# Tying a weight sum behind the previous quad's wide low part in a seven-product matmul block

## The chip, the cores and the metric

The kernel runs on one core of a Trainium2 chip. The metric is the device time of one launch in microseconds (us), the median of several runs. The five engines are named as in the profile: PE (TensorE; its weight loads have a row of their own, PEld), DVE (VectorE), ACT (ScalarE), POOL (GpSimd) and SP, which only issues transfers here.

## The reference

One decoder layer on a sequence of 512 tokens of width 2048, all in float32. What matters for the change is the large input projection of the normalised tokens u, and the output projection of the two branches h_a and h_b:

```python
u = _rmsnorm(h, norm_w)
proj = jnp.matmul(u, w_in)
...
y_a = jnp.matmul(h_a, w_out[:ML_WIDTH])
y_b = jnp.matmul(h_b, w_out[ML_WIDTH:])
return jax.nn.sigmoid(gate_a) * y_a + jax.nn.sigmoid(gate_b) * y_b
```

Between the two stand the mLSTM branch (8 heads) and the gated DeltaNet branch (16 heads), both chunked; the change does not touch them.

## The kernel before, in words

**Split products.** A float32 product is made of three matmuls of a narrower kind: each operand is split into a high part (a cast on ACT, line 140) and a low part (source minus high part, on DVE, line 143), and PE adds high·high, high·low and low·high. So each weight tile passes ACT, then DVE, before PE can finish with it.

**Seven-product blocks.** `seven_stage` (from line 484) computes the product of 512 tokens with 1024 weight columns by a Strassen-Winograd scheme with seven products instead of eight. `SEVEN` lists 13 such blocks of w_in, which run first; `OUTS` lists two of w_out, near the end. A block works through 16 *quads* of weights: A0 to A7 in its first part, B0 to B7 in its second. A quad is one raw tile of three 128x512 weight pieces (`wr3`, three buffers), loaded through SP.

- An A quad needs sums of its pieces (lines 519 and 520 in `first_sums`, on DVE): `t13`, two pieces wide, and `ts`, one piece. `ts` and the first raw piece are split singly (narrow splits), `t13` is split as one tile of 128x1024 (the wide split). `ts` is also sent to DRAM (`t2_d`, line 533, POOL), to come back as the third piece of the B quad with the same number.
- A B quad needs one sum, `ts` (line 537 on DVE), which is split narrowly, and its first two raw pieces are split as the wide tile. The sum waits for all three pieces of the quad.

Of the wide parts (`w2h`, `w2l`) there are two buffers, of `ts` three, of the narrow parts four. In B the products of a quad run in the order m1, m5, m7; m1 and m5 use the wide parts, m7 the narrow ones. Only at a block's end they run B6.m1, B6.m5, B7.m1, B7.m5, B6.m7, B7.m7. Each product is 2 x 3 matmuls (t = 0 and 1; lines 577 to 579).

**Between the parts.** In A the products m6, m1, m5, m7 are gathered in PSUM. When A7 is done with one of them, it is taken out: m6 by ACT (`copy1`, line 562), the others by DVE additions into the tile X (`add`, line 631): U1 = m6 + m1, C22 = U1 + m5, C22 = C22 + m7, each for t = 0 and 1, six additions. B goes on in the banks of m1, m5 and m7, so each product of B0 waits for the addition that reads its bank.

**What sets the order.** PE keeps the order in which the code is written. On the other engines a scheduler orders the instructions by priority and by when it thinks that they are ready; each engine then runs its list strictly in that order, and an instruction that waits holds up everything behind it. `behind("V")` binds an instruction on DVE to come after the newest low part (`newest["V"]`, set in `split_lo`). `prep_sums(q)` writes the sum and the narrow splits of quad q, `prep_pair(q)` its wide split; both are called one quad ahead of the products.

Of the kernel before, what the change touches and what calls it, by code (L numbers as in the profile page):

```python
# [11 lines left out]
ALU = mybir.AluOpType  # L12
# [46 lines left out]
def hybrid_body(  # L59
# [18 lines left out]
    V, A, G, T = nc.vector, nc.scalar, nc.gpsimd, nc.tensor  # L78
# [66 lines left out]
    def behind(eng):  # L145

        return tc.issue_after(newest[eng])
# [332 lines left out]
    def seven_stage(sbp, su, s4, X, t2_d, w_, k0, blocks, sinks, hook, queue):  # L480
# [26 lines left out]
        def split(src, wide):  # L507
            if wide:
                hi, lo = (sbp.tile([P, 2, NO], F32R, tag=f"w2{n}", name=f"w{n}", bufs=2) for n in "hl")
            else:  # L510
                hi, lo = (wp.tile([P, 1, NO], F32R, tag=f"w{n}", name=f"w{n}", bufs=NSPL) for n in "hl")
            split_hi(hi, src)
            split_lo(lo, src, hi)
            return [(hi[:, n, :], lo[:, n, :]) for n in range(2 if wide else 1)]

        def first_sums(r):
            ts = wp.tile([P, 1, NO], F32, tag="tg", name="ts", bufs=3)
            t13 = sbp.tile([P, 2, NO], F32, tag="t13", name="t13")
            V.tensor_tensor(out=t13, in0=r[:, 1:3, :], in1=r[:, 0:2, :], op=ALU.subtract)
            V.tensor_tensor(out=ts[:, 0, :], in0=r[:, 2, :], in1=t13[:, 0, :], op=ALU.subtract)  # L520
            return ts, t13

        def prep_sums(q):

            if q >= len(quads) or q in partq:
                return
            _, c1, c2, b, g, i = quads[q]
            r = rawq[q]
            with tc.high_priority(offset=2 * PRIO):
                if g == "A":  # L530
                    ts, t13 = sums.pop(q) if q in sums else first_sums(r)
                    p_ = split(ts, False)
                    queue.dma_start(t2_d[b % 2, i], ts[:, 0, :])  # L533
                    partq[q] = (p_ + split(r[:, 0:1, :], False), t13)
                else:
                    ts = wp.tile([P, 1, NO], F32, tag="tg", name="ts", bufs=3)
                    V.tensor_tensor(out=ts[:, 0, :], in0=r[:, 0, :], in1=r[:, 2, :], op=ALU.subtract)  # L537
                    partq[q] = (split(ts, False), r[:, 0:2, :])

        def prep_pair(q):  # L540
# [23 lines left out]
        def seven(n0, kind, c1, c2):  # L564
# [20 lines left out]
            for n in range(N - 2):  # L585
                prep_sums(n0 + n + 1)
                prep_pair(n0 + n + 1)
                load_quad()
                for m in range(4 if n < KH else 3):
                    if n == N - 3 and m == 2:  # L590
                        prep_sums(n0 + N - 1)
                        prep_pair(n0 + N - 1)
                    product(n, m)
# [3 lines left out]
            for n, m in ((N - 2, 0), (N - 2, 1), (N - 1, 0), (N - 1, 1), (N - 2, 2), (N - 1, 2)):  # L597
                if (n, m) == (N - 2, 1):
                    prep_sums(n0 + N)
                if (n, m) == (N - 1, 0):  # L600
                    prep_pair(n0 + N)
                    load_quad()
                if last and (n, m) == (N - 1, 1):
                    hook()
                product(n, m)
# [1159 lines left out]
```

## Time and profile before

| | us |
|---|---|
| median of 3 runs | 2181.37 (2178.75 to 2184.76) |
| the profiled execution, its own time | 2172.99 |
| its span, first to last instruction | 2171.2 |
| first seven-product matmul of the 13 blocks | 124.1 |
| first seven-product matmul of the two blocks of w_out | 1957.6 |

The granted clock of PE was 0.999 over the span. In the lines that follow, PEld rows are weight loads of PE, one ahead of each matmul; a row of the timeline has start, duration, engine, line, operation, written tile <- read tiles and shape, and in brackets how long the engine sat idle before it and what ended that. Rows of waits have the sum in us, the number of waits and the longest. All times of the traces are counted from the first instruction.

### The profile page before, as it was taken

What the parts mean: (1) busy time and instruction counts of PE and PEld (TensorE: products, weight loads), DVE (VectorE), ACT (ScalarE), POOL (GpSimd) and SP (SyncE); (2) the same over time, 40 slices, a digit from 0 to 9 for tenths busy, and PEclk for the clock granted to TensorE, in tenths of its full rate; (3) what the DMA queues carried; (4) which work ended last, traced back from release to release, by engine and by line L of the source; (5) the groups of instructions that cost most, each with busy time, mean ns of one, the idle gap of its engine ahead of it and who ended that gap; (6) DMA issues with size and microseconds to landing.
All of it is one profiled execution on the core that took longest, in us unless ns stands there. A gap on an engine that the chain in (4) does not pass through costs nothing. (4 is left out here: it accounts for less than half of the span.)

```text
span 2171.2 us, 31926 instructions
## 1 busy us (share of the span) xinstructions
PE 2131.3 (98%) x10544; PEld 1756.0 (81%) x10544; DVE 1715.0 (79%) x2973; ACT 1035.5 (48%) x1994; POOL 432.0 (20%) x651
## 2 busy tenths in 40 slices
PE   6999999999999999999999999999999999999998
PEld 5888888888788887878878888888888888887786
DVE  5887788788788778777866887887887878668877
ACT  5444444444444444444445546456455464435345
POOL 0000000000004000000003335234243263243211
PEclk9999999999999999999999999999999999999999
DMA  5456676667668766766766767677686677778886
GB/s 160 124 185 202 195 213 199 213 199 226 198 222 245 242 191 219 242 186 222 257 197 172 196 173 184 169 181 185 178 222 171 165 185 209 198 239 266 232 281 242
DMA packets 447143, 444.20 MB, mean 205 GB/s; under 512 B 197121, under 2 KB 303842, under 8 KB 446850
## 3 DMA queue, kind: packets, MB, share of 16 engines
q1 hardware_dynamic: 377618, 337.22, 54.1%
q0 software_dynamic: 24752, 72.90, 10.8%
q10 hardware_dynamic: 44608, 32.06, 4.6%
q8 instruction: 82, 1.34, 0.3%
q14 instruction: 83, 0.68, 0.1%
HBM read 348.66 MB, written 97.58 MB: 206 GB/s over the span
## 5 line engine op out<-in xcount | busy, mean ns | idle before, releaser
L140 ACT CAST wh<-wr 128x512 fp32r<-128x512 f32 (+1 forms) x522 | 373.2, 717 | 415.4 <-PE pj L258 231.4
L143 DVE TENSOR_TENSOR wl<-wr,wh 128x512 fp32r<-128x512 f32 (+1 forms) x522 | 437.4, 840 | 109.3 <-ACT wh L140 103.7
L257 PE MATMUL pj<-uh,wh 128*128 128x512 f32 x896 | 376.0, 420 | 0.0
L259 PE MATMUL pj<-uh,wl 128*128 128x512 f32 x896 | 350.8, 391 | 0.0
L258 PE MATMUL pj<-ul,wh 128*128 128x512 f32 x896 | 350.2, 391 | 0.0
L578 PE MATMUL ps<-wl,uh 128*128 128x512 f32 x752 | 295.0, 392 | 4.8 <-DVE wl L143 4.8
L577 PE MATMUL ps<-wh,uh 128*128 128x512 f32 x752 | 294.5, 392 | 4.1 <-DVE X L631 3.5
L579 PE MATMUL ps<-wh,ul 128*128 128x512 f32 x752 | 292.8, 389 | 0.0
L140 ACT CAST wh<-ts 128x512 fp32r<-128x512 f32 x240 | 148.2, 617 | 250.9 <-DVE ts L537 197.8
L140 ACT CAST wh<-t 128x1024 fp32r<-128x1024 f32 x120 | 126.4, 1054 | 275.7 <-PE ps L579 165.7
L577 PE MATMUL ps<-wh,suh 128*128 128x512 f32 x624 | 242.9, 389 | 1.5 <-ACT to L642 1.5
L533 POOL DMA_DIRECT2D t_d<-ts x104 | 56.6, 544 | 936.9 <-DVE ts L520 883.0
L578 PE MATMUL ps<-wl,suh 128*128 128x512 f32 x624 | 242.8, 389 | 0.0
L579 PE MATMUL ps<-wh,sul 128*128 128x512 f32 x624 | 242.7, 389 | 0.0
L259 PEld LDWEIGHTS pj<-uh,wl 128*128 128x128 f32 x896 | 168.3, 188 | 37.3
L257 PEld LDWEIGHTS pj<-uh,wh 128*128 128x128 f32 x896 | 169.0, 189 | 30.0
L258 PEld LDWEIGHTS pj<-ul,wh 128*128 128x128 f32 x896 | 169.2, 189 | 28.1
L143 DVE TENSOR_TENSOR wl<-ts,wh 128x512 fp32r<-128x512 f32 x240 | 163.7, 685 | 35.2 <-ACT wh L140 35.2
L143 DVE TENSOR_TENSOR wl<-t,wh 128x1024 fp32r<-128x1024 f32 x120 | 146.8, 1224 | 55.9 <-ACT wh L140 55.0
L578 PEld LDWEIGHTS ps<-wl,uh 128*128 128x128 f32 x752 | 141.1, 188 | 40.7 <-DVE wl L143 12.7
L577 PEld LDWEIGHTS ps<-wh,uh 128*128 128x128 f32 x752 | 141.1, 188 | 40.1 <-DVE X L631 10.8
L537 DVE TENSOR_TENSOR ts<-wr 128x512 f32<-128x512 f32 x120 | 82.8, 690 | 104.2 <-DMA wr<-t_d 86.1
(334 smaller groups left out, 3826.2 us busy)
## 6 DMA issues: line engine op xcount, KB each, us to landing
wr<-in_w_in_dram SPq DMA_DIRECT2D x744, 256.0 KB, 3.8
wr<-in_w_out_dram SPq DMA_DIRECT2D x138, 256.0 KB, 5.0
t_d<-ts POOLq DMA_DIRECT2D x104, 256.0 KB, 3.9
wr<-t_d SPq DMA_DIRECT2D x104, 256.0 KB, 3.9
xt<-in_x_dram SPq DMA_DIRECT2D x8, 512.0 KB, 7.1
tg_d<-X ACTq DMA_DIRECT2D x16, 256.0 KB, 6.9
tg_d<-to ACTq DMA_DIRECT2D x16, 256.0 KB, 6.0
v<-v_d SPq DMA_DIRECT2D x8, 512.0 KB, 5.8
```

The costliest lines, as they stand in the source:

```text
L140: newest["A"] = A.copy(hi, src).ins
L143: newest["V"] = V.tensor_tensor(out=lo, in0=src, in1=hi.bitcast(F32), op=ALU.subtract).ins
L257: T.matmul(ps[j], hi[:, k, wsl], uh[:, kt, :], start=(kt == 0), stop=False)
L258: T.matmul(ps[j], hi[:, k, wsl], ul[:, kt, :], start=False, stop=False)
L259: T.matmul(ps[j], lo[:, k, wsl], uh[:, kt, :], start=False, stop=(kt == KT - 1))
L533: queue.dma_start(t2_d[b % 2, i], ts[:, 0, :])
L537: V.tensor_tensor(out=ts[:, 0, :], in0=r[:, 0, :], in1=r[:, 2, :], op=ALU.subtract)
L577: T.matmul(ps[t], ah, hi, start=(g == "A" and i == 0), stop=False, skip_group_check=True)
L578: T.matmul(ps[t], ah, lo, start=False, stop=False, skip_group_check=True)
L579: T.matmul(ps[t], al, hi, start=False, stop=(i == KH - 1), skip_group_check=True)
```

## The change

The line that sums the pieces of a B quad is put under `behind("V")`. When it is written, the newest low part is that of the wide split of the quad in front of it (of A7 for B0, of B0 for B1, and so on), so the sum can no longer come ahead of that one in DVE's list.

```diff
                 else:
                     ts = wp.tile([P, 1, NO], F32, tag="tg", name="ts", bufs=3)
-                    V.tensor_tensor(out=ts[:, 0, :], in0=r[:, 0, :], in1=r[:, 2, :], op=ALU.subtract)
+                    with behind("V"):
+                        V.tensor_tensor(out=ts[:, 0, :], in0=r[:, 0, :], in1=r[:, 2, :], op=ALU.subtract)
                     partq[q] = (split(ts, False), r[:, 0:2, :])
```

The lists of PE and SP stay word for word the same (line numbers behind the sum grow by one: the sum is L538 after, the addition L632). On POOL one load of stage-two gates changes places with one load of the last block's operand. On DVE and ACT rows move in each of the 15 blocks, and nowhere else.

DVE from the end of A to the start of B in the third block, before. The raw tiles wr3_2737, wr3_2783, wr3_2821 and wr3_2867 are the quads B0, B1, B2 and B3; X_517 is the tile of the six additions:

```order
L537 TENSOR_TENSOR ts_2857<-wr3_2783 128x512
L143 TENSOR_TENSOR wl_2860<-ts_2857,wh_2859 128x512
L143 TENSOR_TENSOR wl_2818<-wr3_2737,wh_2817 128x1024
L537 TENSOR_TENSOR ts_2889<-wr3_2821 128x512
L631 TENSOR_TENSOR X_517<-X_517,ps_2468 128x512
L631 TENSOR_TENSOR X_517<-X_517,ps_2469 128x512
L631 TENSOR_TENSOR X_517<-X_517,ps_2470 128x512
L143 TENSOR_TENSOR wl_2892<-ts_2889,wh_2891 128x512
L631 TENSOR_TENSOR X_517<-X_517,ps_2471 128x512
L631 TENSOR_TENSOR X_517<-X_517,ps_2472 128x512
L537 TENSOR_TENSOR ts_2921<-wr3_2867 128x512
L631 TENSOR_TENSOR X_517<-X_517,ps_2473 128x512
```

The same place on DVE, after:

```order
L143 TENSOR_TENSOR wl_2818<-wr3_2737,wh_2817 128x1024
L538 TENSOR_TENSOR ts_2857<-wr3_2783 128x512
L632 TENSOR_TENSOR X_517<-X_517,ps_2468 128x512
L632 TENSOR_TENSOR X_517<-X_517,ps_2469 128x512
L632 TENSOR_TENSOR X_517<-X_517,ps_2470 128x512
L143 TENSOR_TENSOR wl_2860<-ts_2857,wh_2859 128x512
L632 TENSOR_TENSOR X_517<-X_517,ps_2471 128x512
L632 TENSOR_TENSOR X_517<-X_517,ps_2472 128x512
L632 TENSOR_TENSOR X_517<-X_517,ps_2473 128x512
L143 TENSOR_TENSOR wl_2864<-wr3_2783,wh_2863 128x1024
L538 TENSOR_TENSOR ts_2889<-wr3_2821 128x512
L143 TENSOR_TENSOR wl_2896<-wr3_2821,wh_2895 128x1024
```

Before, the sum of B2 stood ahead of the six additions and the sum of B3 among them; now only B1's sum is ahead of them, and B1's wide low part follows right behind them.

ACT at the same place, before (copies of line 562 are `copy1`):

```order
L140 CAST wh_2813<-ts_2811 128x512
L140 CAST wh_2859<-ts_2857 128x512
L140 CAST wh_2817<-wr3_2737 128x1024
L562 COPY X_517<-ps_2466 128x512
L562 COPY X_517<-ps_2467 128x512
L140 CAST wh_2891<-ts_2889 128x512
```

ACT at the same place, after:

```order
L140 CAST wh_2813<-ts_2811 128x512
L140 CAST wh_2817<-wr3_2737 128x1024
L563 COPY X_517<-ps_2466 128x512
L563 COPY X_517<-ps_2467 128x512
L140 CAST wh_2859<-ts_2857 128x512
```

The cast of B1's sum stood ahead of B0's wide cast and of the two copies; now it is behind them.

DVE at the end of the same block, before. wr3_2963, wr3_2995 and wr3_3027 are B6, B7 and the next block's A0:

```order
L537 TENSOR_TENSOR ts_3043<-wr3_2995 128x512
L143 TENSOR_TENSOR wl_3046<-ts_3043,wh_3045 128x512
L143 TENSOR_TENSOR wl_3024<-wr3_2963,wh_3023 128x1024
L519 TENSOR_TENSOR t13_3070<-wr3_3027 128x1024
L520 TENSOR_TENSOR ts_3069<-wr3_3027,t13_3070 128x512
L143 TENSOR_TENSOR wl_3050<-wr3_2995,wh_3049 128x1024
```

The same place, after:

```order
L143 TENSOR_TENSOR wl_3024<-wr3_2963,wh_3023 128x1024
L538 TENSOR_TENSOR ts_3043<-wr3_2995 128x512
L519 TENSOR_TENSOR t13_3070<-wr3_3027 128x1024
L143 TENSOR_TENSOR wl_3046<-ts_3043,wh_3045 128x512
L520 TENSOR_TENSOR ts_3069<-wr3_3027,t13_3070 128x512
L143 TENSOR_TENSOR wl_3050<-wr3_2995,wh_3049 128x1024
```

The sum of B7 and its narrow low part, which were ahead of B6's wide low part, now stand behind it, between it and B7's own.

## The prediction

> **What bounds the kernel now.** I read the page first, then the waits of the weight loads, then the timeline where these waits fall. First the busy time of PE and of its weight loads, and three groups of the page: the matmul group whose mean I use, and the two groups of weight loads that wait.
>
> ```profile
> span 2171.2 us, 31926 instructions
> PE 2131.3 (98%) x10544; PEld 1756.0 (81%) x10544; DVE 1715.0 (79%) x2973; ACT 1035.5 (48%) x1994; POOL 432.0 (20%) x651
> ...
> L579 PE MATMUL ps<-wh,sul 128*128 128x512 f32 x624 | 242.7, 389 | 0.0
> ...
> L578 PEld LDWEIGHTS ps<-wl,uh 128*128 128x128 f32 x752 | 141.1, 188 | 40.7 <-DVE wl L143 12.7
> L577 PEld LDWEIGHTS ps<-wh,uh 128*128 128x128 f32 x752 | 141.1, 188 | 40.1 <-DVE X L631 10.8
> ```
>
> PE is taken all the time, and PEld, too, has only 19% of the span free. How fast a block runs when nothing is late shows in the windows view of the weight loads for one of the 13 blocks (columns: stretch, its length, busy time and count, clock, DMA share, GB/s):
>
> ```profile
> 742.00:818.00 76.00, 62.90 (x336) 1.00 0.68 220
> ```
>
> A block is 336 matmuls, so this one ran in 76.0 us, 0.226 us from load to load, of which a load takes 0.19 and 0.04 is the usual gap. A matmul takes 0.389 us by its row, so consecutive ones overlap. Now who makes the blocks wait, first by matmuls, then by weight loads (sum in us, count, longest):
>
> ```profile
> PE ps L578 <- DVE wl L143: 5.2, 12, 0.9
> PE ps L577 <- DVE X L631: 3.5, 6, 1.4
> ```
>
> ```profile
> PEld ps L578 <- DVE wl L143: 13.5, 23, 1.4
> PEld ps L577 <- DVE X L631: 11.5, 18, 1.9
> ```
>
> The two differ by almost three. A matmul counts as busy until its modelled end, 0.389 us, though the next could follow after 0.226; a wait shorter than 0.16 us vanishes, and a longer one loses 0.16. The loads show every one, so I sum by them. The Trainium skill, Perfetto Trace Analysis, section Identifying the Most-Contended Engine, says that matmul busy time is a poor measure of headroom, since matmuls are pipelined, and names LDWEIGHTS busy time instead; the trace agrees (98% against 81%). By the matmul rows the whole prize would be 5.2 + 3.5 = 8.7 us, by the load rows 22.6, as follows.
>
> The share in the second parts of the blocks: the additions (X, line 631) hold up only B0, so all 11.5 us. Of the low parts, the products with `uh` hold 12.7 of the 13.5. Together 24.2 us, less the usual gap of 0.04 us in up to 41 waits, 1.6: **22.6 us**. PE is the resource that sets the end from the first block on, so what goes there goes from the time, unless it returns later.
>
> Why is DVE late, at 79% busy? Its own waits say (of the sum, line 537):
>
> ```profile
> DVE ts L537 <- DMA wr<-t_d: 86.1, 63, 3.7
> ...
> DVE ts L537 <- DMA wr<-t2o_d: 15.4, 11, 3.4
> ```
>
> In 74 of 120 cases the sum stands at the head of DVE's list and waits for the quad's third piece to come back from DRAM, 101.5 us in all, and everything behind it waits too: also the wide low part of the quad ahead, whose data are there and which PE needs sooner. Here is the step from A to B in the third block, on PEld, DVE and ACT:
>
> ```profile
> 321.46 0.19 PEld L579 LDWEIGHTS ps<-wh,sul 128*128 128x128 f32 x1
> 322.15 0.19 PEld L577 LDWEIGHTS ps<-wh,uh 128*128 128x128 f32 x1 [0.51 <-DVE X L631]
> ...
> 324.55 0.19 PEld L577 LDWEIGHTS ps<-wh,s4h 128*128 128x128 f32 x1 [0.49 <-DVE X L631]
> ...
> 326.41 0.19 PEld L577 LDWEIGHTS ps<-wh,uh 128*128 128x128 f32 x1 [0.63 <-DVE X L631]
> ...
> 327.55 0.19 PEld L578 LDWEIGHTS ps<-wl,uh 128*128 128x128 f32 x1 [0.38 <-DVE wl L143]
> ```
>
> ```profile
> 316.39 0.69 DVE L537 TENSOR_TENSOR ts<-wr 128x512 f32<-128x512 f32 x1 [0.89 <-DMA wr<-t_d]
> 317.85 0.69 DVE L143 TENSOR_TENSOR wl<-ts,wh 128x512 fp32r<-128x512 f32 x1 [0.76 <-ACT wh L140]
> 318.80 1.22 DVE L143 TENSOR_TENSOR wl<-wr,wh 128x1024 fp32r<-128x1024 f32 x1 [0.26 <-ACT wh L140]
> 320.81 0.69 DVE L537 TENSOR_TENSOR ts<-wr 128x512 f32<-128x512 f32 x1 [0.79 <-DMA wr<-t_d]
> 321.42 1.88 DVE L631 TENSOR_TENSOR X<-X,ps 128x512 f32<-128x512 f32 x3
> 323.21 0.68 DVE L143 TENSOR_TENSOR wl<-ts,wh 128x512 fp32r<-128x512 f32 x1
> 323.82 1.28 DVE L631 TENSOR_TENSOR X<-X,ps 128x512 f32<-128x512 f32 x2
> 325.06 0.69 DVE L537 TENSOR_TENSOR ts<-wr 128x512 f32<-128x512 f32 x1
> 325.68 0.68 DVE L631 TENSOR_TENSOR X<-X,ps 128x512 f32<-128x512 f32 x1
> 326.27 1.22 DVE L143 TENSOR_TENSOR wl<-wr,wh 128x1024 fp32r<-128x1024 f32 x1
> ```
>
> ```profile
> 317.19 0.62 ACT L140 CAST wh<-ts 128x512 fp32r<-128x512 f32 x1 [3.31 <-DVE ts L537]
> 317.72 1.05 ACT L140 CAST wh<-wr 128x1024 fp32r<-128x1024 f32 x1
> 318.67 1.06 ACT L562 COPY X<-ps 128x512 f32<-128x512 f32 x2
> ...
> 322.12 1.04 ACT L140 CAST wh<-wr 128x1024 fp32r<-128x1024 f32 x1
> ```
>
> The B1 sum waits until 316.39; ACT's cast of it (317.19) stands ahead of B0's wide cast (317.72) and of both copies (318.67). Then the B2 sum waits until 320.81 ahead of the six additions, and the B3 sum stands among them (325.06). PE waits at each: 0.51 + 0.49 + 0.63 + 0.38 = 2.01 us, less four gaps of 0.04: 1.85 lost in this block.
>
> **The change at the start of B.** Nothing is added or taken away; the same operations stand in another order. I follow the third block in its new order, with steps from these rows: a DVE operation of 512 columns every 0.60 us (three in 1.88, the last 0.68), one of 1024 every 1.14, a wide cast 1.05 and the next ACT operation 0.95 after its start. A wide cast starts when PE has let go of its buffer, 0.66 us after the last weight load that used it (321.46 to 322.12).
>
> A7 starts 23 loads before 321.46, at 316.26, so A6's last load is at 316.03, and B0's wide cast starts at 316.69 instead of 317.72; the copies follow at 317.64. DVE: wide low of B0 at 317.8, B1's sum at 318.9 (its data came at 316.4), the first three additions at 319.5, 320.1, 320.7, B1's narrow low part at 321.3, the other additions at 321.9, 322.5, 323.1 (end 323.8), B1's wide low at 323.7, end 324.95 (its cast, bound by PE, ends at 323.16 as now). PE without waits starts B0 at 321.69 and takes a t every 0.68; it needs the six additions at 321.69, 322.37, ... 325.09, each 0.68 later, and they end 0.9 to 1.6 ahead. B1's low part is due at 325.99, 1.0 after it is ready. So all four waits go, not only those that a sum ended; next late would be the additions, if DVE came 0.9 us later.
>
> What is now behind the sum in question: B1's narrow low part and B2's sum (323.21 before) start some 2 us later, but m7, third in its quad, uses them. The three copies of raw quads are freed by the wide low parts, which come earlier, so the loads through SP start earlier as well; SP's list is unchanged. On ACT only casts change places. On POOL two loads near the end change places; I count that at nothing, since both belong to work further on, and its bound either way is under 1 us.
>
> **Later in B.** A wide low part is now paced by PE: its quad's predecessor but one loads m5's last weights 11 loads (2.5 us) after its start, then 0.66, 1.05, and 1.22: ready 5.4 us after that start, 2.7 us before it is needed. The sum follows it, and by then its data, released one wide low part earlier, have had two quads' time. At the block's end the order has a price. Block ten, on DVE, and the wait of B7 on PEld:
>
> ```profile
> 883.41 1.23 DVE L143 TENSOR_TENSOR wl<-wr,wh 128x1024 fp32r<-128x1024 f32 x1 [0.26 <-ACT wh L140]
> ...
> 886.93 1.22 DVE L143 TENSOR_TENSOR wl<-wr,wh 128x1024 fp32r<-128x1024 f32 x1 [0.26 <-ACT wh L140]
> 889.10 1.23 DVE L519 TENSOR_TENSOR t<-wr 128x1024 f32<-128x1024 f32 x1 [0.94 <-DMA wr<-in_w_in_dram]
> ...
> 890.97 1.22 DVE L143 TENSOR_TENSOR wl<-wr,wh 128x1024 fp32r<-128x1024 f32 x1
> ```
>
> ```profile
> 892.24 0.19 PEld L578 LDWEIGHTS ps<-wl,uh 128*128 128x128 f32 x1 [0.88 <-DVE wl L143]
> ```
>
> The wide low parts are B5, B6, B7's. B5's frees the tile for the next block's A0 at 884.64; 4.46 us later L519 can start. B7's low part was due at 892.24 - 0.84 = 891.40. By the pace above B5's would be ready at 881.7 (B5 starts at 884.4), 2.9 earlier; A0 lands at 886.1, DVE does B6's wide low (end 885.8), B7's sum, L519 at 886.4, B7's narrow low, L520, B7's wide low at 888.8, end 890.0: 1.4 us ahead. The wait goes here too. In the first block of w_out it does not:
>
> ```profile
> 2024.16 1.22 DVE L143 TENSOR_TENSOR wl<-wr,wh 128x1024 fp32r<-128x1024 f32 x1
> ...
> 2032.54 1.23 DVE L519 TENSOR_TENSOR t<-wr 128x1024 f32<-128x1024 f32 x1 [1.82 <-DMA wr<-in_w_out_dram]
> ```
>
> ```profile
> 2035.69 0.19 PEld L578 LDWEIGHTS ps<-wl,uh 128*128 128x128 f32 x1 [1.35 <-DVE wl L143]
> ```
>
> There the load took 7.16 us from release (2025.38); released 0.7 earlier, but with one more step of 0.60 ahead of B7's wide low part, it leaves the 1.3 us as they are.
>
> **The sum.** 22.6 - 1.3 = 21.3 us, 2172.99 - 21.3 = 2151.7 for the profiled execution. The median of the runs shown is 8.4 us above that execution; taken off it, 2181.4 - 21.3 = **2160**. If the 8.4 us are such waits too, which no row shows, the gain is up to 29.7.
>
> **Rivals.** *The block's end takes part back.* A0's load lands no earlier than now (more loads bunch), and B7's narrow low part adds its 0.60 in each of 14 block ends: 21.3 - 8.4 = 12.9 gained, 2168.5. If the waits at block ends stay as well, bounded by 12.7 less B1's share (0.34 x 15 = 5.1), 7.6, the gain is 22.6 - 8.4 - 7.6 = 6.6, 2174.8. For it speaks block ten's 0.94; against it, that the release comes 2.9 earlier. Chance 0.12.
>
> *Too few buffers.* The wait at B1 recurs in the same place of every block, and the wide parts have only two buffers: if PE's release of A7's buffer set it, no order on DVE would help, and the additions would merely move: 2181, no change. Against it: B1's wide cast ended at 323.16, its low part began at 326.27, 3.1 us of DVE's list. The Trainium skill, Perfetto Trace Analysis, section Optimization Strategy, says that consistent bubbles can mean too little SBUF for the next tile; by that rule the change would be idle; these two rows speak against it. Chance 0.10.
>
> *Slower.* The end of a block now hangs on A0's load through two more DVE operations. By block ten, L519 must start by 887.7, that is 6.0 us after the release at 881.7; every us more costs 14. At 7.5 us the gain is gone, from 8.0 the kernel is slower by over 0.3%, and at 9 us, twice block ten's, it loses 42 - 21 = 21 us: 2202. For it: 7.16 in the block of w_out. Against: 4.46 in block ten. Chance 0.05.
>
> That the order would stay the same is ruled out by the lists.
>
> **How the numbers follow.** The forecast has 0.73, the rivals 0.12, 0.10, 0.05. The range goes from 2181.4 - 29.7 = 2152 to the first rival's far end, 2174; it leaves out the last two. A measurement of this kernel can tell about 0.3% (6.5 us) from no change; beyond it faster are the forecast and most of the first rival, 0.83; within it 0.12; slower 0.05.
>
> **What would show it.** In the changed kernel PEld's waits for X (line 632 there) fall from 11.5 us to under 1, those for `wl` from 13.5 to under 4; the sum's waits for DMA fall well below 101.5; in each block B1's wide low part ends before PE is due. Waits for `wl` at B7 that grow would prove the block's end right; waits for X that stay, with DVE idle before wide low parts until ACT's casts, the buffers. A gain without these waits going would prove the reasoning wrong.

## The result and the profile after

| | before | after |
|---|---|---|
| median of 4 runs each, us | 2183.07 (2178.75 to 2184.82) | 2154.74 (2153.08 to 2157.67) |
| the profiled execution, its own time | 2172.99 | 2153.58 |

The ratio of the times is 0.9878, 95% interval 0.986 to 0.9896: the change gains 28.3 us, 1.2%. Between the two profiled executions it is 19.4 us. These two numbers differ, and the first question below is why. One execution of `tie_b1` (below) took 3060.36 us at a granted clock of 0.656 and is left out of its numbers.

The page after, the rows that answer to those of before (the sum is line 538 now, the products 578 to 580):

```profile
span 2151.8 us, 31880 instructions
PE 2122.0 (99%) x10544; PEld 1759.9 (82%) x10544; DVE 1709.4 (79%) x2973; ACT 1042.1 (48%) x1994; POOL 431.0 (20%) x651
...
L579 PEld LDWEIGHTS ps<-wl,uh 128*128 128x128 f32 x752 | 141.2, 188 | 29.5 <-DVE wl L143 0.2
L578 PEld LDWEIGHTS ps<-wh,uh 128*128 128x128 f32 x752 | 141.2, 188 | 29.2
```

The same number of loads, busy for as long as before, with 29.5 and 29.2 us of idle time ahead of them in place of 40.7 and 40.1; that is 22 us less in these two groups. What the seven-product stages and the stage ahead of the blocks of w_out (`py`) still wait for, by the waits of the loads after:

```profile
PEld ps L578 <- DVE X L1412: 2.6, 3, 1.9
...
PEld py L1389 <- DVE wl L143: 1.7, 1, 1.7
...
PEld ps L579 <- DVE wl L143: 0.7, 2, 0.5
...
PEld ps L578 <- ACT to L643: 0.3, 1, 0.3
```

No row is left for the six additions (line 632), and `wl` has 0.7 us in two waits where it had 13.5 in 23. On DVE the sum does not wait for a DMA at all any more: 101.5 us in 74 waits went to none. DVE's idle time did not go away, though; it moved. First before, then after, DVE's waits in front of low parts:

```profile
DVE wl L143 <- ACT wh L140: 194.2, 245, 4.3
```

```profile
DVE wl L143 <- ACT wh L140: 282.0, 300, 3.0
```

DVE is busy for as long as before (1709.4 against 1715.0 us) and now spends its free time where the next low part waits for its cast, and the cast for PE to let go of a buffer: 87.8 us more there (ACT's casts themselves wait 307.2 us for PE at line 580; before, at 579, it was 248.7). That is idle time of an engine that is ahead.

The third block as a whole, after and before, from its first load to the next block's first (columns: stretch, length, busy time and count, clock, DMA share, GB/s):

```profile
277.23:353.39 76.16, 63.08 (x337) 1.00 0.68 206
```

```profile
278.17:355.85 77.68, 62.67 (x337) 1.00 0.67 203
```

76.16 us for 336 matmuls is 0.2267 each; the load rows of the timeline stand just that far apart, so PE has nothing left to wait for in this block. Its step from A to B, on DVE, ACT and PEld:

```profile
316.82 1.23 DVE L143 TENSOR_TENSOR wl<-wr,wh 128x1024 fp32r<-128x1024 f32 x1 [1.77 <-ACT wh L140]
317.96 0.68 DVE L538 TENSOR_TENSOR ts<-wr 128x512 f32<-128x512 f32 x1
318.56 1.87 DVE L632 TENSOR_TENSOR X<-X,ps 128x512 f32<-128x512 f32 x3
320.36 0.68 DVE L143 TENSOR_TENSOR wl<-ts,wh 128x512 fp32r<-128x512 f32 x1
320.96 1.87 DVE L632 TENSOR_TENSOR X<-X,ps 128x512 f32<-128x512 f32 x3
322.75 1.22 DVE L143 TENSOR_TENSOR wl<-wr,wh 128x1024 fp32r<-128x1024 f32 x1
323.89 0.68 DVE L538 TENSOR_TENSOR ts<-wr 128x512 f32<-128x512 f32 x1
```

```profile
315.73 1.05 ACT L140 CAST wh<-wr 128x1024 fp32r<-128x1024 f32 x1 [1.75 <-PE ps L580]
316.68 1.06 ACT L563 COPY X<-ps 128x512 f32<-128x512 f32 x2
```

```profile
320.75 0.19 PEld L578 LDWEIGHTS ps<-wh,uh 128*128 128x128 f32 x1
...
325.05 0.19 PEld L579 LDWEIGHTS ps<-wl,uh 128*128 128x128 f32 x1
```

B0 starts at 320.75; B1's low part is ready at 322.75 + 1.22 = 323.97 and is loaded at 325.05, 1.08 us later. None of the loads in between has a wait in brackets. DVE runs from 316.82 to the end of the second sum without a gap.

### The profile page after: what moved, and what is told of

Its sections match the earlier page's. It is cut to its first block, busy times and chain, and to the rows that moved or that the text cites. A ratio compares the mean times of both kernels' runs of the same rounds, so it can differ in the third digit from the quotient of the medians.

```text
span 2151.8 us, 31880 instructions
## 1 busy us (share of the span) xinstructions
PE 2122.0 (99%) x10544; PEld 1759.9 (82%) x10544; DVE 1709.4 (79%) x2973; ACT 1042.1 (48%) x1994; POOL 431.0 (20%) x651
## 5 line engine op out<-in xcount | busy, mean ns | idle before, releaser
L258 PEld LDWEIGHTS pj<-ul,wh 128*128 128x128 f32 x896 | 169.4, 189 | 28.2
L580 PEld LDWEIGHTS ps<-wh,ul 128*128 128x128 f32 x752 | 141.2, 188 | 29.5
L579 PEld LDWEIGHTS ps<-wl,uh 128*128 128x128 f32 x752 | 141.2, 188 | 29.5 <-DVE wl L143 0.2
L578 PEld LDWEIGHTS ps<-wh,uh 128*128 128x128 f32 x752 | 141.2, 188 | 29.2
```

What stands on the lines that cost most here:

```text
L258: T.matmul(ps[j], hi[:, k, wsl], ul[:, kt, :], start=False, stop=False)
L578: T.matmul(ps[t], ah, hi, start=(g == "A" and i == 0), stop=False, skip_group_check=True)
L579: T.matmul(ps[t], ah, lo, start=False, stop=False, skip_group_check=True)
L580: T.matmul(ps[t], al, hi, start=False, stop=(i == KH - 1), skip_group_check=True)
```

## The experiments

The theory was that of the prediction: a sum that waits for its quad's third piece at the head of DVE's list holds up the wide low parts and the additions behind it, and PE waits for those. The rivals were: that the place in the order matters and not the wait; that only the step from A to B counts, or that the rest of B has a share of its own; that the trip through DRAM is the cause; and that the block's end takes something back. Each time is set against runs of the kernel before on the same chip; a difference between two changed kernels of different chips is called so, and is to be read with the 1.5 to 5.6 us over which four runs of one such kernel spread.

**The kernel before once more, twice.** Its edit is none.

> The kernel before, unchanged, for another profiled execution. The recorded one took 2172.99 us, 8 to 10 under the median of the others. If the rest of the measured gain (28 us against 21.3 forecast) is the same kind of wait, an execution of about 2182 us shows PEld waits on X and wl some 8 us longer than the 25.0 of the recorded one, with the stretches outside the seven-product blocks unchanged within 2 us. Rival: the waits stay near 25 us and the extra time lies outside the blocks or after the last instruction.

> The kernel before once more, for a third profiled execution. The second took 4.7 us longer than the first and its PEld waits on X and wl were 2.8 us longer (27.8 against 25.0). If such waits make the spread of its times, waits and time go together again: about 25 us of waits at 2173, 28 at 2178, over 30 at 2182. Rival: no connection.

They took 2177.72 and 2181.79 us. The waits of the loads in the second one:

```profile
PEld ps L578 <- DVE wl L143: 17.4, 26, 1.4
...
PEld ps L577 <- DVE X L631: 11.9, 20, 1.8
...
PEld ps L577 <- ACT to L642: 2.8, 3, 1.5
PEld ps L577 <- DVE X L1411: 2.6, 3, 1.9
...
PEld py L1388 <- DVE wl L143: 2.3, 2, 1.7
PEld ps L577 <- ACT wh L140: 1.1, 2, 0.6
```

Low parts and additions together: 25.0 us in the execution recorded first (2172.99), 27.8 in the first repeat (2177.72), 29.3 in the second (2181.79). The kernel before varies from run to run (2172 to 2187 over all chips), and the waits vary with it, but at about 2182 us by 4.3 us, half of the 8 that were expected. Where the rest lies shows when the executions are cut at the first and the last load of the blocks (us, from the timelines):

| stretch | before, recorded | first repeat | second repeat | after |
|---|---|---|---|---|
| ahead of the blocks of w_in | 124.1 | 125.1 | 125.2 | 124.9 |
| 13 blocks of w_in | 1005.8 | 1008.1 | 1011.6 | 990.3 |
| from there to the blocks of w_out | 827.7 | 828.4 | 829.8 | 828.4 |
| two blocks of w_out | 160.5 | 161.2 | 160.3 | 155.0 |
| behind them | 53.2 | 53.1 | 53.2 | 53.1 |

Of the 8.8 us between the recorded execution and the second repeat, 5.6 lie in the blocks and 3.2 outside them, where at most 2 had been expected. Against the second repeat, after is 2181.79 - 2153.58 = 28.2 us faster, 26.6 of it in the blocks. All six rows are 38.1 us here in 56 waits, the four of after 5.3 in 7; without the rows of `py`, which lies outside the blocks, 35.8 in 54 and 3.6 in 6. So 48 waits with 32.2 us of idle time went, and the blocks became 26.6 shorter: a wait counts for its idle time less about 0.12. Against an execution near the median, most of the 28 us are thus waits in the blocks, while the 19.4 came of the comparison with one of the fastest executions of before. This rests on one such execution.

**Nearly the same order, with and without the wait.** `tie_two` ties the sum behind the wide low part two quads ahead, not one:

```diff
-        rawq, partq, sums = [], {}, {}
+        rawq, partq, sums, wides = [], {}, {}, {}
...
-                    V.tensor_tensor(out=ts[:, 0, :], in0=r[:, 0, :], in1=r[:, 2, :], op=ALU.subtract)
+                    with tc.issue_after(wides[q - 2]):
+                        V.tensor_tensor(out=ts[:, 0, :], in0=r[:, 0, :], in1=r[:, 2, :], op=ALU.subtract)
...
+                wides[q] = newest["V"]
```

> The sum is tied behind the wide low part two quads ahead instead of one: nearly the order of before, with B2's sum ahead of the additions and waiting for its data, only B3's sum out of them. Theory (the sum's wait for data at the head of DVE's list holds up the work behind it): most of the loss stays, 2170 to 2180 us. Rival (any tie helps, since it evens out the order): near 2155.

`free_sum2` is `tie_two` with a sum whose operands are in SBUF from the start:

```diff
+                    with tc.issue_after(wides[q - 2]):
+                        V.tensor_tensor(out=ts[:, 0, :], in0=uh[:, 0, :].bitcast(F32), in1=uh[:, 1, :].bitcast(F32), op=ALU.subtract)
```

> The order of tie_two, but the sum of a B quad reads two tiles that lie in SBUF since the start instead of the quad, so that it waits for no transfer (its values are not those of the reference; every operation, transfer and matmul stays). Theory (the wait does the harm, not the place): PEld waits on X and wl fall below 4 us, 2153 to 2160 us. Rival (the sum's work ahead of the additions does it): like tie_two, 2170 to 2180.

`tie_two`: 2171.84, ratio 0.9959 (0.9943 to 0.9975). `free_sum2`: 2153.98, ratio 0.9882 (0.986 to 0.9904), with B2's sum in the same place, behind B0's wide low part and ahead of the additions, and on the same chip. The waits of the loads, `tie_two` first:

```profile
PEld ps L580 <- DVE wl L143: 13.8, 25, 1.5
PEld ps L579 <- DVE X L633: 8.6, 12, 1.9
```

```profile
PEld ps L579 <- DVE X L633: 0.6, 1, 0.6
PEld ps L580 <- DVE wl L143: 0.5, 1, 0.5
```

The same operations, 17.9 us apart. The lists of PE are the same; on DVE the scheduler did not keep quite the same order. In the third block of `free_sum2` B1's sum stands three places further forward and B4's one; in some later blocks an addition or a low part has moved, too. In the third block neither move takes a sum out of the way of a step that PE needs: the sums of B1 and B2 are still ahead of the additions, and yet that block takes 76.16 us where it took 77.67. So at these places it is the sum's wait for data that costs, and not DVE's work for it; what the small difference of order adds over all blocks was not separated. And two buffers of wide parts are enough, since they were two in both.

**The step from A to B, and the rest of B.** `tie_start` ties the sums of B0 to B3 only, `tie_rest` those of B4 to B7 only:

```diff
+                    with behind("V") if i < 4 else ExitStack():
```

> The tie for B0 to B3 only; B4 to B7 as before. Theory (most of the loss lies in the step from A to B): waits on X gone, waits on wl only at B5 to B7, about 4 us, time 2157 to 2163 us. Rival (the later quads carry half of it): 2165 to 2172.

```diff
+                    with behind("V") if i >= 4 else ExitStack():
```

> The tie for B4 to B7 only; B0 to B3 as before. Theory (the step from A to B makes the loss, and the waits at B4 to B7 follow from it): 0 to 5 us under before. Rival (each quad's tie brings its share): 10 to 14 us under before.

`tie_start`: 2154.14, ratio 0.9886 (0.9862 to 0.9909), all that the change gains and more than was expected. `tie_rest`: 2172.22, ratio 0.9965 (0.9953 to 0.9977), 9.0 us gained, more than the 0 to 5 that were expected and less than the rival's 10 to 14. Together 25.7 + 9.0 = 34.7 us, more than the 28.3 of both at once. That the two overlap is likely and not shown by the times, since the three intervals together leave room for some 7 us. The traces fit it: part of what is lost in the later quads seems to follow from a late start of B. With `tie_start`, whose later sums are not tied, `wl` keeps 2.2 us in 5 waits, all at B6 and B7, where before had 4.5 in 7 at B5 to B7. The additions, in `tie_rest`, still wait as before:

```profile
PEld ps L578 <- DVE X L632: 10.4, 14, 3.4
```

**Which sum of the step.** `tie_b1` ties B1's alone, `tie_b23` those of B2 and B3:

```diff
+                    with behind("V") if i == 1 else ExitStack():
```

> The tie for B1 alone: its sum and cast go behind B0's wide low part and the two copies; B2's sum stays ahead of the six additions and waits for its data, B3's among them. Theory (B2's wait ahead of the additions does most of the harm): 2168 to 2180. Rival (B1's sum, by holding up B0's wide cast and the copies on ACT): 2155 to 2162.

```diff
+                    with behind("V") if i in (2, 3) else ExitStack():
```

> The tie for B2 and B3 alone: nothing is left ahead of the additions but B1's sum, which still comes ahead of B0's wide cast and the copies. Theory: most of the gain, 2154 to 2162, since B1's data come some 3 us before the additions. Rival (B1's place matters as much): 2165 to 2172.

`tie_b1` is the surprise: ratio 1.0132 (1.01 to 1.0163), 2208.1 to 2210.6 us against 2181.08, 29 us slower than before, where both the theory and the rival had it faster. One tie of the eight costs as much as all of them gain. DVE in its third block, and two loads of B0 on PE:

```profile
325.23 1.23 DVE L143 TENSOR_TENSOR wl<-wr,wh 128x1024 fp32r<-128x1024 f32 x1 [2.05 <-ACT wh L140]
326.37 0.68 DVE L538 TENSOR_TENSOR ts<-wr 128x512 f32<-128x512 f32 x1
328.50 0.69 DVE L538 TENSOR_TENSOR ts<-wr 128x512 f32<-128x512 f32 x1 [1.45 <-DMA wr<-t_d]
329.11 1.28 DVE L632 TENSOR_TENSOR X<-X,ps 128x512 f32<-128x512 f32 x2
...
333.90 1.22 DVE L143 TENSOR_TENSOR wl<-wr,wh 128x1024 fp32r<-128x1024 f32 x1
335.04 0.68 DVE L632 TENSOR_TENSOR X<-X,ps 128x512 f32<-128x512 f32 x1
```

```profile
329.84 0.19 PEld L578 LDWEIGHTS ps<-wh,uh 128*128 128x128 f32 x1 [0.72 <-DVE X L632]
...
335.77 0.19 PEld L578 LDWEIGHTS ps<-wh,uh 128*128 128x128 f32 x1 [1.21 <-DVE X L632]
```

B0's wide low part now comes first, as wanted, but the scheduler put B1's and B2's sums one behind the other ahead of the additions. The second waits 1.45 us, and all six additions stand behind it; PE waits 0.72 us for the first of them. The Trainium skill, PSUM — Partial Sum Buffer, section Engine vs sequencer instructions, says that the queues of ScalarE, VectorE and GpSimd are strict FIFO; the trace agrees, with these 1.45 us in front of additions that do not need the sum. But the wait is only a part of it: B2's sum waited ahead of the additions before, too (0.79 us). Before, one narrow low part and B3's sum stood among the additions; here it is two narrow low parts, B3's sum and, ahead of the sixth addition, B1's wide low part (333.90). So the last of them starts 335.04 - 329.11 = 5.9 us after the first, where it was 4.3, and PE waits 1.21 for it. Over the run the waits of the loads for X grow to 37.8 us and those for `wl` to 24.9. How much of the 29 us is the wait and how much the order of the work was not separated.

`tie_b23`, the other way about: 2158.14, ratio 0.9899 (0.9879 to 0.992). B1's sum still stands ahead of B0's wide low part, and the six additions run in one piece:

```profile
318.97 3.67 DVE L632 TENSOR_TENSOR X<-X,ps 128x512 f32<-128x512 f32 x6
```

No wait for X is left there, and 4.9 us for `wl`. Tying the sums of B2 and B3, which stood ahead of the additions and among them, takes 22.9 us of the loss away. For the prediction's first reason, B1's sum and its cast ahead of B0's, little is left: 3 to 5 us against `tie_start` and the whole change, and both are on other chips.

**How much room the new order has.** `dose1` and `dose2` are the change with one or two DVE operations of 1024 columns more in each block, behind B0's wide low part:

```diff
+        def added(t, m1):
+            if t == 0:
+                with behind("V"):
+                    add(sbp.tile([P, 2, NO], F32, tag="t13", name="t13"), uh[:, 0:2, :].bitcast(F32), uh[:, 2:4, :].bitcast(F32))
+                with behind("V"):
+                    add(X[:, 1, :, :], uh[:, 0:2, :].bitcast(F32), uh[:, 2:4, :].bitcast(F32))
+            add(U1[t], U1[t], m1[t])
```

(the second `with` only in `dose2`; B1's wide low part is bound behind the additions in both, so that the order stays.)

> The changed kernel with one more DVE operation of 128x1024 (1.14 us) behind B0's wide low part in every block, ahead of the six additions; the order behind it is held as in the changed kernel. Its result goes to a tile that is free then, so nothing else changes. Theory (DVE has about 1.0 us to spare there: B1's wide low part is ready 1.09 us ahead in the changed kernel's trace): 0.1 us lost a block, 0 to 3 us over the changed kernel. Rival (DVE is the bound at this place, or has far more to spare): 17 us over it, or nothing.

> As dose1 with two such operations, 2.28 us in every block. Theory (slack about 1.09 us): 2.28 - 1.09 = 1.2 us lost in each of 15 blocks, 18 us over the changed kernel, about 2173. Rival (bound already): 34 us over it; rival (slack far larger): nothing.

`dose1`: 2157.25, ratio 0.9897 (0.9878 to 0.9917). `dose2`: 2171.03, ratio 0.9955 (0.994 to 0.997). The first operation, 1.14 us in each of 15 blocks, costs 2.5 us over the median of after on another chip, no more than runs scatter (0 to 3 were expected); the second costs 13.8 more on the same chip, 0.92 in each block, and brings the kernel 16.3 over after, where 18 were expected. By the traces, the third block takes 76.23 us with one operation and 77.33 with two, 0.07 and 1.17 more than after: just about what 1.14 and 2.28 us exceed B1's margin of 1.08 by. The waits of the loads in `dose2`:

```profile
PEld ps L586 <- DVE X L640: 18.7, 30, 0.9
...
PEld ps L587 <- DVE wl L143: 6.8, 18, 1.8
```

30 waits for X are two in each of 15 blocks. One operation fits into the room, two do not: the room is about one operation, as the forecast's margin of 1.0 for B1's low part said. Its 0.9 for the additions was too small: with 1.14 us more no load waits for X in `dose1`.

**Without the trip through DRAM.** `no_trip` loads the third piece of a B quad from the weights, not from what POOL stored:

```diff
-                src = (w_[k2, c1:c1 + NO], w_[k2, c2:c2 + NO], t2_d[b % 2, i])
+                src = (w_[k2, c1:c1 + NO], w_[k2, c2:c2 + NO], w_[k1, c2:c2 + NO])
```

> The kernel before, but the third piece of a B quad is loaded from w_in (w_out) and not from the sum that was sent to DRAM (its values are not those of the reference); the lists of PE, DVE, ACT and POOL are the same. Theory (the sum waits because the load starts only when a wide low part frees the raw tile, not because of the way through DRAM): within 4 us of before, and the sum still waits some 100 us for its loads. Rival (the way through DRAM makes it late): 15 to 28 us under before.

2177.65, ratio 0.9989 (0.9978 to 1.0): about nothing. The sum waits as before:

```profile
DVE ts L537 <- DMA wr<-in_w_in_dram: 82.5, 59, 4.4
DVE ts L537 <- DMA wr<-in_w_out_dram: 17.7, 10, 4.0
```

100.2 us against 101.5. So the third piece is not late because it comes back from DRAM. SP shows what its load waits for; these are the loads of B2 in the third block of before:

```profile
314.93 0.91 SPq L505 DMA_DIRECT2D wr<-in_w_in_dram  x2
315.93 0.38 SPq L505 DMA_DIRECT2D wr<-t_d  x1
```

They start when the last low part of the raw tile's former quad, A7, has ended (314.22 + 0.68 = 314.90), the third piece is issued last of the three, and B2's sum starts 4.9 us after that, at 320.81. That earlier release of the raw tiles would alone be enough was not tried.

**The block's end.** `untie_last` is the change without the tie of B7, so that the next block's A0 is not behind one operation more:

```diff
+                    with behind("V") if i < KH - 1 else ExitStack():
```

> The changed kernel with the tie left out for B7 alone, so that its sum and narrow low part stand ahead of B6's wide low part again and not between it and B7's. Theory (that place costs 0.6 us only where the next block's A0 comes late, and there is room for it): the time is that of the changed kernel within 3 us, 2152 to 2158. Rival (the block's end gives part of the gain back): 4 to 8 us under the changed kernel.

2153.97, ratio 0.99 (0.9878 to 0.9921), against 2154.74 for the change on another chip: no difference, and the 13 blocks of w_in take 990.3 us in both traces. The block's end takes nothing back.

## Why the prediction was right, and where it was off

The forecast was 2160 us in a range from 2152 to 2174, and 2154.7 came, near the range's lower end. The signs that it named are there: the waits for X and `wl` went (none and 0.7 us), the sum waits for no DMA, and no load waits for B1's wide low part.

**The step from A to B: right, row by row.** The third block begins 0.94 us earlier than before (277.23 against 278.17). Taking that off the forecast's times, with the measured ones beside them: B0's wide cast 315.75 and 315.73; the copies 316.70 and 316.68; B0's wide low 316.86 and 316.82; B1's sum 317.96 and 317.96; the first additions 318.56 and 318.56; B1's narrow low 320.36 and 320.36; B1's wide low 322.76 and 322.75; B0 on PE 320.75 and 320.75. The margins: B1's low part 1.08 ahead (forecast 1.0); the additions end at 319.24, 319.84, 320.43, 321.64, 322.24 and 322.83, that is 1.2 to 1.7 ahead of 320.75, 321.43 and so on by 0.68. The forecast said 0.9 to 1.6, which was a slip of its subtraction: its own times, 320.2 against 321.69 and so on, give 1.2 to 1.7 as well. Such a replay can be done by hand where every engine's order is known and the durations come from the trace.

**Block ends in w_in: right.** Block ten, after, on DVE (the low parts of B5, B6 and B7 and the next A0's sum) and PEld (B7's first low part):

```profile
870.62 1.23 DVE L143 TENSOR_TENSOR wl<-wr,wh 128x1024 fp32r<-128x1024 f32 x1 [0.87 <-ACT wh L140]
...
874.71 1.23 DVE L143 TENSOR_TENSOR wl<-wr,wh 128x1024 fp32r<-128x1024 f32 x1 [0.87 <-ACT wh L140]
...
876.45 1.22 DVE L519 TENSOR_TENSOR t<-wr 128x1024 f32<-128x1024 f32 x1
...
878.79 1.22 DVE L143 TENSOR_TENSOR wl<-wr,wh 128x1024 fp32r<-128x1024 f32 x1
```

```profile
881.54 0.19 PEld L579 LDWEIGHTS ps<-wl,uh 128*128 128x128 f32 x1
```

L519 starts without waiting for its DMA, B7's low part is ready at 880.01, 1.53 us ahead (forecast 1.4).

**The block of w_out: mis-sized.** The prediction said that the new order "leaves the 1.3 us as they are". After:

```profile
2006.53 1.23 DVE L143 TENSOR_TENSOR wl<-wr,wh 128x1024 fp32r<-128x1024 f32 x1 [1.15 <-ACT wh L140]
...
2013.76 1.23 DVE L519 TENSOR_TENSOR t<-wr 128x1024 f32<-128x1024 f32 x1 [1.60 <-DMA wr<-in_w_out_dram]
```

```profile
2017.37 0.19 PEld L579 LDWEIGHTS ps<-wl,uh 128*128 128x128 f32 x1 [0.25 <-DVE wl L143]
2017.48 0.19 PEld L580 LDWEIGHTS ps<-wh,ul 128*128 128x128 f32 x1
```

The wait is 0.25 less the gap of 0.04, 0.21. The load took 2013.76 - 2007.76 = 6.0 us from the release, where the 7.16 of before had been carried over. A duration of a DMA from one place of one execution is the weakest row of such a replay.

**The sum for the profiled execution: 21.3 forecast, 19.4 measured.** The step that was off is the price of a wait, "I sum by them". In the last two rows the load after the late one comes 0.11 us later and not 0.2267: the loads catch up by about 0.11 behind each wait. The same in before, behind the fourth wait of the third block (327.55, shown above):

```profile
327.65 0.19 PEld L579 LDWEIGHTS ps<-wh,ul 128*128 128x128 f32 x1
327.88 0.19 PEld L577 LDWEIGHTS ps<-wh,uh 128*128 128x128 f32 x1
```

So here a wait costs its idle time less about 0.15, not less 0.04. In the third block the forecast had 1.85 us lost; by the two windows it is 77.68 - 76.16 = 1.52. Over the 15 blocks the loads sat idle 25.9 us less in 39 waits fewer, and the blocks became 20.9 us shorter: 0.13 less for each wait. Of these 20.9, the second parts of the blocks, which alone the forecast had priced, gave 19.0 of its 21.3. Two terms that the forecast had at nothing nearly cancel. The first parts became 1.9 us shorter, mostly by A0's wait for ACT's line 642 (1.9 us in the recorded execution, 0.3 after); that row has 1.9 to 2.8 us in the four traces with the old order (`no_trip` among them) and from none to 1.9 in the others, so a part of it may come from the change. The stretches outside the blocks became 1.5 longer: the blocks begin 0.8 later, and 0.7 were lost between those of w_in and those of w_out, where `py` waits 1.7 us after, and not at all in the recorded execution of before, but 2.3 in its second repeat. 19.0 + 1.9 - 1.5 = 19.4. So the mechanism was right, its price was about 2 us too high, and that the whole comes as near as it does is in part luck. By matmul rows it would have been 8.7, by load rows 22.6; the prediction's choice of the loads was the right one: by the matmul rows the forecast would have been less than half of what came. The Trainium skill's rule in Perfetto Trace Analysis, section Identifying the Most-Contended Engine, had pointed the same way.

**The median: 2160 forecast, 2154.7 measured.** The forecast left the 8.4 us between the recorded execution and the median in place, and named the other case: "if the 8.4 us are such waits too, which no row shows, the gain is up to 29.7". That other case is, for the most part, what happened: by the second repeat, 5.6 of 8.8 us are time in the blocks (table above). The 2160 itself rested on leaving them in place, for which no row spoke either.

**The reasons.** "To come back from DRAM" fell (`no_trip`); being the last piece, landing late, stands. "Next late would be the additions, if DVE came 0.9 us later" was wrong: in `dose1`, 1.14 us later, no load waits for them. In `dose2`, 2.28 us later, they and B1's low part are both late (18.7 us, and 4.1 of the 6.8 for `wl`). That B1's sum was to blame for the first wait is only half so: with B1's sum in its old place (`tie_b23`) 22.9 us are gained, and tying it alone costs 29.

**The rivals.** *The block's end* fell: `untie_last` is no faster. *Too few buffers* fell with the change itself and with `free_sum2`. The Trainium skill (Perfetto Trace Analysis, section Optimization Strategy) says that consistent bubbles can mean too little SBUF; here they meant something else: the wait at B1, 13 times in the 15 blocks of the recorded execution, went with the same buffers. *Slower* needed A0's sum to start more than 6.0 us after the release; in block ten it started 876.45 - 871.85 = 4.6 after, and in the block of w_out at just 6.0, where the first small wait shows. Its threshold fits that one place, and it was not far off.

## What to carry to other kernels

Here an operation that waited for a transfer at the head of an in-order list cost what stood behind it, not what it does itself: look at what the waiting engine's next instructions are for and move the waiting one behind those that the bound engine needs sooner. Then look at the list that comes out: a tie on one such operation put other work among the steps that PE needs, and cost as much as ties on all of them gain. If the runs spread more than the effect you look for, profile the kernel before more than once, and price PE's waits by the loads with what they catch up taken off.

## What had not been expected

The loads' catching up, about 0.11 us behind a wait, was not in the forecast. Neither was how far the kernel before spreads, up to 13 us on one chip (2173.94 to 2186.62, 16 runs). The four runs of after spread over 4.6 us and the four of before beside them over 6.1, so whether the change also steadies the kernel is not shown. The tie of B1 alone, 29 us slower, shows how far apart two orders of the same instructions can be: 2210 and 2154 us, 2.6%.
